# Order and costs in a planned lead-in: one transformer layer on one Trainium2 core

## The chip, the cores and the metric

The kernel runs on one core of one Trainium2 chip. The metric is the device time of one execution in microseconds; the time before is 1137.44 us, the median of 3 runs (1137.27 to 1139.29). The engines are named as the profile names them: PE (TensorE, matmuls), PEld (its weight loads), DVE (VectorE), ACT (ScalarE), POOL (GpSimd) and SP (SyncE, which issues nearly all DMAs here).

## The reference

One layer over 256 latent tokens and 256 context tokens of width 2048, in float32:

```python
sh1, sc1, g1, sh2, sc2, g2 = ada_mods(c, w_ada, b_ada)          # silu(c) @ w_ada + b_ada, in six parts
csh1, csc1, ... = ada_mods(c_ctx, w_ada, b_ada)
qa, ka, va, qb, kb, vb = mixer_qkv(x * (1 + sc1) + sh1, w_in, ...)      # one 2048 x 3072 projection, rope
qac, kac, vac, qbc, kbc, vbc = mixer_qkv(ctx * (1 + csc1) + csh1, w_in, ...)
heads = concat([window_sink_attention(qa, ka, va, kac, vac, sink),      # 8 heads, window 128, sink logit
                global_attention(qb, kb, vb, kbc, vbc)])                # 8 heads, normalised q and k
x = layer_norm(ALPHA * x + g1 * (heads @ w_out), ln1_g, ln1_b)
x = layer_norm(ALPHA * x + g2 * swiglu(x * (1 + sc2) + sh2, w_gate, w_up, w_down), ln2_g, ln2_b)
```

The feed-forward part has a hidden width of 5632. `w_ada` is 2048 x 12288, `w_in` 2048 x 3072.

## The kernel before

**Products in three parts.** Every large product is made of three matmuls on rounded float32 (`mm3`, L331 to L333): weights and activations are each split into a high part (a cast on ACT) and a low part (the rest, a subtraction on DVE), and high by high, low by high and high by low are added up in one PSUM bank. In the planned part the weights' high part is made in line L593 and the low part in L596; for the first group of activations the high part `uh` is made in L757, the whole value `uf` in L762, and the low part `ul` in L772.

**The planned part.** From the start to the beginning of the feed-forward part the program's order isn't written by hand. Each step (a DMA issue, a cast, a group of matmuls, a copy) is given to the class `Flow` with its engine, an assumed duration, the steps that it comes after, and the buffers that it takes and gives back. `Flow.search` orders the steps: it runs the list forward with ranks, gets new ranks from a backward pass, changes ranks at random (`SEED`, `MOVES`), and scores an order by `replay`, which plays it with the assumed durations and with `DRAWS` sets of durations scattered by `JITTER`. The best order is written out, one queue for each engine. On the chip each engine works through its queue in that order and waits only where data or a buffer requires it; a dependency that stands only in the plan makes no wait, only an order. The durations that matter here are `dma_ns` (L550, the rate of a load by the length of its rows), the casts (L598) and the attention's products with the values (L1097).

**The input product by groups.** The 2048 rows of `w_in` are taken in `GROUPS` of 1, 1, 2, 4 and 8 slices of 128 rows. Each group needs its columns of shift and scale first: `flow_columns` loads those columns of `w_ada` for the shift and the scale, PE multiplies them with the conditioning (L644), ACT copies the sums (L674), PE adds up the four partial rows (L679), and DVE adds the bias (L687 shift, L689 scale). `flow_part` then turns the activations round on PE (L743) and modulates them. For the first group this is done for the latent tokens (`s` = 0) and for the context (`s` = 1): `high` on ACT (L757), `whole` on DVE (L762), `rest` on DVE (L772).

`flow_blocks` loads the group's weights. A group of one slice has four pieces, of 512, 1024, 1024 and 512 columns: block 2 (keys and values of heads A, four row tiles of 128 tokens, so twelve matmuls), blocks 0 and 1, blocks 3 and 4 (queries, two row tiles each), and block 5 (keys and values of heads B). The first group's pieces go to buffers of their own (pool `b4`), all later weights to six raw buffers of 1 MB, which the columns of `w_ada` share. A raw buffer comes free when its `lo` step (L596) or its product (L644) is done, and only then can SP issue the next load for it. Around these steps PE does short products on an identity (`warm`, L381).

**After the plan** come the feed-forward loops over `w_gate` and `w_up` and over `w_down`, in an order that the tile framework keeps from the source.

Of the kernel before, what the change touches and what calls it, by code (L numbers as in the profile page):

```python
# [36 lines left out]
NB = 512  # L37
# [32 lines left out]
class Flow:  # L70
# [6 lines left out]
    OTHER = {"SP": 2000, "PE": 270, "ACT": 90, "DVE": 90, "POOL": 150}  # L77
    AGAIN = 1300
    ROUNDS = 8
    SEED, SIGMA, MOVES, DRAWS, JITTER = 312, 600.0, 800, 4, 0.03  # L80

    def __init__(self, room, begin):
        self.room, self.begin, self.steps, self.at = dict(room), begin, [], 0.0
# [173 lines left out]
def dit_layer(ctx: ExitStack, tc: tile.TileContext, x, c, cx, c_ctx, w_ada, b_ada, w_in, q_norm_g,  # L257
# [4 lines left out]
    w_ada, w_in, w_out, w_gate, w_up, w_down = (w[0] for w in (w_ada, w_in, w_out, w_gate, w_up, w_down))  # L262
# [99 lines left out]
    araw = ea.enter_context(tc.tile_pool(name="araw", bufs=ADA_BUFS))  # L362
# [146 lines left out]
    def const_tables():  # L509
        nc.gpsimd.tensor_scalar_mul(nsink, sinkb, -1.0)  # L510
        for t in range(NT):
            for g, cg, sg in ((gq, cosQ, sinQ), (gk, cosK, sinK)):
# [18 lines left out]
    F = Flow({"raw": RAW_BUFS, "araw": ADA_BUFS, "hl": HL_BUFS, "acc": 4, "wk": 4, "b4": NB4, "t2k": T2K},  # L531
             {"SP": 1800.0, "PE": 6300.0, "ACT": 5100.0, "DVE": 4200.0, "POOL": 4000.0})
# [12 lines left out]
    kv_room = [[Buf("b4") for _ in range(2)] for _ in range(2)]  # L545
# [2 lines left out]
        room.pool = "b4"  # L548

    def dma_ns(nbytes, row):  # L550
        return nbytes / (390 if row >= 2048 else 340 if row >= 1024 else 290)

    def flow_load(w, k0, nk, c0, width, where=("raw", "araw"), cut=1, small=False):
        room = Buf(*where)
# [20 lines left out]

        return room, F.add("SP", dma_ns(nk * width * P * 4, width * 4), fn, take=[room])

    def flow_weights(w, k0, nk, c0, width=NB, where=("raw", "araw"), spare=False, small=False):

        raw, ld = flow_load(w, k0, nk, c0, width, where, small=small)  # L580
        pieces = []
        for s in range(0, nk * width, SUB * NB):
            n = min(SUB * NB, nk * width - s)
            hl = Buf("b4" if spare else "hl")
            hl.rooms = [hl, Buf("b4")] if spare else [hl]

            def cast(hl=hl, s=s, n=n):
                if spare:
                    hl.hi, hl.lo = (b4([P, SUB * NB], F32R, c) for c in ("hi", "lo"))
                else:  # L590
                    hl.hi = whl.tile([P, SUB * NB], F32R, tag="hi", name="hi")
                    hl.lo = whl.tile([P, SUB * NB], F32R, tag="lo", name="lo")
                nc.scalar.copy(hl.hi[:, :n], raw.t[:, s : s + n])  # L593

            def rest(hl=hl, s=s, n=n):
                nc.vector.tensor_tensor(hl.lo[:, :n], raw.t[:, s : s + n], hl.hi[:, :n].bitcast(F32), op=ALU.subtract)  # L596

            a = F.add("ACT", 60 + 0.87 * n, cast, [ld], hl.rooms)  # L598
            b = F.add("DVE", 60 + 1.06 * n, rest, [a], give=[raw])
            pieces.append((hl, (a, b)))  # L600
        return pieces

# [26 lines left out]
    last_load, first_sum = [], []  # L629

    def flow_columns(c0, ncol, shift, scale, ats, at):

        width = ncol * P
        nk = G4 * NB // width
        ns = KD // nk
        bank, prev = Buf("wk"), None

        def fn(g, i, raw, k0, k1):
            if g == i == k0 == 0:
                bank.t = wk_bank()  # L640
            for c in range(k0, k1):
                k = g * nk + c
                j = k % 4
                nc.tensor.matmul(  # L644
                    bank.t[32 * j : 32 * j + 32, :width], lhsT=cs[:, 4 * k + 2 - 2 * i : 4 * k + 34 - 2 * i],
                    rhs=raw.t[:, c * width : (c + 1) * width],
                    start=(i == 0 and k < 4), stop=(i == 1 and k >= KD - 4),
                )

        for g in range(ns):  # L650
            F.at = ats[g]
            (r0, l0), (r1, l1) = (flow_load(w_ada, g * nk, nk, c0 + i * D, width, cut=1 if c0 else 4) for i in range(2))
            last_load[:] = [l1]
            if c0:
                def both(g=g, r0=r0, r1=r1):
                    fn(g, 0, r0, 0, nk)
                    fn(g, 1, r1, 0, nk)

                prev = F.add("PE", 1860, both, [l0, l1, prev], [bank] if g == 0 else [], [r0, r1])
            else:  # L660
                def one(i, r):
                    fn(0, i, r, 0, nk)
                    if i:
                        warm(wps.t, 2)

                prev = F.add("PE", 1080, lambda r=r0: one(0, r), [l0, prev], [bank], [r0])
                first_sum.append(prev)
                prev = F.add("PE", 1520, lambda r=r1: one(1, r), [l1, prev], [], [r1])
        F.at = at
        sb, ps = Buf("t2k"), Buf("wk")  # L670

        def copy():
            sb.t = t2k("ada")
            nc.scalar.copy(sb.t[:, :width], bank.t[:, :width])  # L674

        def sums():
            ps.t = wk_bank()
            for j in range(ncol):
                nc.tensor.matmul(ps.t[:, 4 * j : 4 * j + 4], lhsT=sb.t[:, j * P : (j + 1) * P], rhs=sel, start=True, stop=True)  # L679
            if c0 == 0:  # L680
                warm(wps.t, 4)

        def add(i):
            pv = ps.t[:, 0 : 4 * ncol].rearrange("p (j i s) -> p j i s", i=2, s=2)
            bs, bc = (bcol[:, k : k + ncol, None].to_broadcast([P, ncol, 2]) for k in (c0 // P, c0 // P + KD))
            if i == 0:
                nc.vector.tensor_tensor(shift, pv[:, :, 0, :], bs, op=ALU.add)  # L687
            else:
                nc.vector.scalar_tensor_tensor(scale, pv[:, :, 1, :], 1.0, bc, op0=ALU.add, op1=ALU.add)  # L689

        a = F.add("ACT", 60 + 0.82 * width, copy, [prev], [sb], [bank])
        b = F.add("PE", 217 * ncol - 70 if c0 else 1150, sums, [a], [ps], [sb] if c0 else [sb, wps])
        adds = [F.add("DVE", 160, lambda i=i: add(i), [(b, 0 if c0 else 1000)], give=[ps]) for i in range(2)]
        return a, adds

    u = {}
# [10 lines left out]
    def flow_part(k0, n, at, each):  # L707
# [16 lines left out]
        if k0:  # L724
            loads = [F.add("SP", max(ns, 500), load_x), F.add("SP", max(ns, 500), load_cx, take=[cx_room])]
        else:
            loads = first_sum * 2
            cx_room.pool, cx_room.t = "b4", cx0
        for s in range(2):
            F.at = at + (0.8 + 0.1 * s) * each  # L730
# [2 lines left out]
            for j0 in range(0, n, 2):  # L733
                nj = min(2, n - j0)
                ps, uf = Buf("wk"), Buf("t2k")
# [40 lines left out]
                          at=None if k0 else -1.0)  # L776
                if n == 1:
                    a = F.add("ACT", 520, high, [p] + ready, rooms)
                    b = F.add("DVE", 470, whole, [a], [uf], [ps])
                    b = F.add("DVE", 360, rest, [b], give=[uf])  # L780
                    u[k0, s][1].append((a, b))
                    continue
                for j in range(nj):
                    p = F.add("ACT", 460, lambda j=j, f=modulate: f(j), [p] + ready, [uf] if j == 0 else [], [ps])
                a = F.add("ACT", 60 + 240 * nj, cast, [p, *(c for c, _ in u[k0, s][1])], rooms if j0 == 0 else [])
                b = F.add("DVE", 60 + 330 * nj, rest, [a], give=[uf])
# [46 lines left out]
    def flow_blocks(g, bs, where=("raw", "araw")):  # L833

        k0, n = GROUPS[g]
        if n == 1:
            for i, (b0, m) in enumerate(((2, 1), (0, 2), (3, 2), (5, 1))):
                F.at = bs[0] + (bs[1] - bs[0]) * i / 4
                piece, = flow_weights(w_in, k0, 1, b0 * NB, m * NB, where if k0 else ("b4",), small=k0 == 0)
                for j in range(m):  # L840
                    flow_block(g, b0 + j, [(piece, [j * NB])])
            return
        for b in bs:
            chunks = []
            for c in range(0, n, G4):
                F.at = bs[b] + 0.01 * c
                for piece in flow_weights(w_in, k0 + c, min(n, G4), b * NB, NB, where):
                    chunks.append((piece, [0, NB]))
            flow_block(g, b, chunks)
# [142 lines left out]
    def flow_attend(gi, at, each):  # L992

        w, kb = gi // 2, gi % 2
# [3 lines left out]
        for p in range(4):  # L998
# [4 lines left out]
            pT, hx, o_ps = Buf("b4"), Buf("b4"), Buf("wk")  # L1003
# [80 lines left out]
            s = [F.add("PE", 760, lambda i=i, f=scores: f(i), qk, [banks[i]], [*qT[gi][0], *kT[w][0]]) for i in range(2)]  # L1084
            m = [F.add("DVE", 615, lambda i=i, f=largest: f(i), [s[i]]) for i in range(2)]
# [5 lines left out]
            n = [F.add("ACT", 630, lambda i=i, f=weigh: f(i), [r]) for i in range(2)]  # L1091
            g = []
            for i in range(2):
                g.append(F.add("DVE", 615, lambda i=i, f=squares: f(i), [n[i], *g], [hx] if i == 0 else [], [probs[i]]))
            a = F.add("SP", 2000, put, g, give=[hx])
            g = [(F.add("SP", 1300, get, [(a, -LANDING[0])], [pT]), -LANDING[1])]
            v = F.add("PE", 1540, values, g, [o_ps], [pT, *kv_room[w]])  # L1097
            a = F.add("ACT", 300, cast, [v, *oT[gi][1].get(0, [])[:1]], o_rooms if p == 0 else [])
            b = F.add("DVE", 350, rest, [a], give=[o_ps])
            oT[gi][1].setdefault(t, []).extend((a, b))  # L1100
# [183 lines left out]
    a = F.add("SP", 2500, const_loads, [start])  # L1284
    tables = F.add("POOL", 6000, const_tables, [a])
    for g in range(last):
        n = GROUPS[g][1]
# [83 lines left out]
    a = F.add("SP", 1000, ln_loads)  # L1371
    a = F.add("PE", 150, ln_flip, [(a, -SLACK)], [lroom])
# [433 lines left out]
```

## Time and profile before

| | |
|---|---|
| Median of 3 runs | 1137.44 us |
| The profiled execution | 1137.55 us, its span 1135.8 us |
| Instructions | 14062 |
| PE busy | 1112.2 us (98%) |
| DVE busy | 844.4 us (74%) |
| ACT busy | 551.4 us (49%) |
| Mean granted clock of PE | 0.994 |
| DMA | 321.26 MB, 283 GB/s over the span |
| Chain that ended last | PE 93%, DVE 3%, ACT 1%, DMA 1% |

The span runs from the first to the last instruction; the device time contains a little more around it. Busy times are sums over an engine's instructions without overlaps. PE's matmuls are pipelined and their ends are modelled, so that a busy PE isn't PE at its peak: whether PE runs without a break is better seen from the distance between starts. In the timeline, the last bracket of a line tells how long the engine was idle before the instruction and what ended that. "DMA share" is the mean busy share of the core's 16 DMA engines.

### The profile page before, as it was taken

How to read it: one execution, taken by the hardware profiler on the slowest of the kernel's cores; microseconds unless marked ns; L12 is line 12 of the kernel's file. 1: busy time of each engine (PE TensorE's matmuls, PEld its weight loads, DVE VectorE, ACT ScalarE, POOL GpSimd, SP SyncE). 2: the span in 40 equal slices, each digit the busy share in tenths (PEclk: the TensorE clock that was granted, in tenths of full speed). 3: DMA queues.
4: the chain of work that ended last, by engine and by line, in shares of the span. 5: the costliest groups of instructions: out<-in, count | busy, mean ns of one | idle time of the engine just before them, and what ended most of it. 6: DMA issues, size and time to landing. Idle time of an engine off the chain costs nothing.

```text
span 1135.8 us, 14062 instructions
## 1 busy us (share of the span) xinstructions
PE 1112.2 (98%) x5255; PEld 893.2 (79%) x5255; DVE 844.4 (74%) x1070; ACT 551.4 (49%) x795; POOL 41.6 (4%) x82
## 2 busy tenths in 40 slices
PE   7999999999999999999999999999999999999996
PEld 6766678778787778888888888888888888888884
DVE  4753579999999888786777566766766887686576
ACT  3341464877685356444464444444444344343442
POOL 1000050110100000010000000000000000000000
PEclk8999999999999999999999999999999999999998
DMA  9999999877999779999977677677677798887541
GB/s 292 377 379 378 377 357 361 288 249 233 336 337 377 272 261 349 317 311 328 313 213 236 224 232 241 215 256 244 226 250 254 263 376 299 315 307 261 187 148 74
DMA packets 178318, 321.26 MB, mean 283 GB/s; under 512 B 8733, under 2 KB 43197, under 8 KB 175944
## 3 DMA queue, kind: packets, MB, share of 16 engines
q1 hardware_dynamic: 177528, 320.03, 81.2%
q8 instruction: 41, 0.67, 0.2%
q10 hardware_dynamic: 720, 0.33, 0.1%
q14 instruction: 29, 0.23, 0.1%
HBM read 304.07 MB, written 16.25 MB: 282 GB/s over the span
## 4 chain that ended last, share of the span: by engine, by line
PE 93%; DVE 3%; ACT 1%; DMA 1%; issue 0%; ACTq 0%; SPq 0%; DVEq 0%
PE acc L331 28%; PE acc L333 28%; PE acc L332 28%; PE wk L644 2%; PE wk L1068 2%; PE wk L743 1%; PE wk L331 1%; DVE hx L1050 1%; PE wk L333 1%; PE wk L332 1%; DMA raw<-in_w_in_dram 1%; DMA cxt<-in_ctx_dram 0%; DVE lo L596 0%; PE wk L1401 0%; PE wk L475 0%
## 5 line engine op out<-in xcount | busy, mean ns | idle before, releaser
L322 DVE TENSOR_TENSOR lo<-raw,hi 128x1024 fp32r<-128x1024 f32 x258 | 312.8, 1221 | 167.5 <-ACT hi L321 165.0
L321 ACT CAST hi<-raw 128x1024 fp32r<-128x1024 f32 x258 | 271.7, 1055 | 335.1 <-PE acc L333 304.3
L331 PE MATMUL acc<-hi,u2h 128*128 128x512 f32 x704 | 274.6, 390 | 1.4 <-ACT u2h L1580 1.4
L333 PE MATMUL acc<-hi,u2l 128*128 128x512 f32 x704 | 274.0, 389 | 0.0
L332 PE MATMUL acc<-lo,u2h 128*128 128x512 f32 x704 | 273.9, 389 | 0.0
L331 PEld LDWEIGHTS acc<-hi,u2h 128*128 128x128 f32 x704 | 132.2, 188 | 28.8 <-ACT u2h L1580 1.6
L333 PEld LDWEIGHTS acc<-hi,u2l 128*128 128x128 f32 x704 | 132.1, 188 | 28.2 <-DVE u2l L1581 0.6
L332 PEld LDWEIGHTS acc<-lo,u2h 128*128 128x128 f32 x704 | 132.2, 188 | 27.1
L331 PE MATMUL acc<-hi,hTh 128*128 128x512 f32 x344 | 133.8, 389 | 0.4 <-ACT acc L1731 0.4
L332 PE MATMUL acc<-lo,hTh 128*128 128x512 f32 x344 | 133.9, 389 | 0.0
L333 PE MATMUL acc<-hi,hTl 128*128 128x512 f32 x344 | 133.8, 389 | 0.0
L593 ACT CAST hi<-raw 128x1024 fp32r<-128x1024 f32 (+1 forms) x86 | 87.5, 1030 | 93.0 <-DMA raw<-in_w_in_dram 42.8
L456 DVE SCALAR_TENSOR_TENSOR adav<-raw,cs,adav 128x512 f32<-128x512 f32 (+1 forms) x128 | 121.3, 947 | 11.0 <-DMA raw<-in_w_ada_dram 7.7
L596 DVE TENSOR_TENSOR lo<-raw,hi 128x1024 fp32r<-128x1024 f32 (+1 forms) x86 | 101.7, 1195 | 18.3 <-ACT hi L593 17.5
L331 PE MATMUL acc<-hi,uh 128*128 128x512 f32 x256 | 105.0, 410 | 1.0 <-ACT uh L757 1.0
L332 PE MATMUL acc<-lo,uh 128*128 128x512 f32 x256 | 101.1, 395 | 1.0 <-DVE lo L596 1.0
L333 PE MATMUL acc<-hi,ul 128*128 128x512 f32 x256 | 101.1, 395 | 0.8 <-DVE ul L772 0.8
L331 PEld LDWEIGHTS acc<-hi,hTh 128*128 128x128 f32 x344 | 64.6, 188 | 14.2 <-ACT acc L1731 0.8
L333 PEld LDWEIGHTS acc<-hi,hTl 128*128 128x128 f32 x344 | 64.6, 188 | 13.5
L332 PEld LDWEIGHTS acc<-lo,hTh 128*128 128x128 f32 x344 | 64.6, 188 | 13.5 <-DVE lo L322 0.2
L331 PEld LDWEIGHTS acc<-hi,uh 128*128 128x128 f32 x256 | 48.9, 191 | 20.4 <-issue 6.1
L333 PEld LDWEIGHTS acc<-hi,ul 128*128 128x128 f32 x256 | 48.6, 190 | 12.3 <-DVE ul L772 1.7
(224 smaller groups left out, 1147.9 us busy)
## 6 DMA issues: line engine op xcount, KB each, us to landing
raw<-in_w_ada_dram SPq DMA_DIRECT2D x70, 1024.0 KB, 6.8
raw<-in_w_gate_dram SPq DMA_DIRECT2D x44, 1024.0 KB, 5.3
raw<-in_w_up_dram SPq DMA_DIRECT2D x44, 1024.0 KB, 5.3
raw<-in_w_down_dram SPq DMA_DIRECT2D x44, 1024.0 KB, 6.5
raw<-in_w_ada_dram SPq DMA_DIRECT2D x48, 512.0 KB, 4.8
raw<-in_w_in_dram SPq DMA_DIRECT2D x18, 1024.0 KB, 6.2
raw<-in_w_out_dram SPq DMA_DIRECT2D x16, 1024.0 KB, 9.1
pd<-hx SPq DMA_DIRECT2D x64, 128.0 KB, 2.7
```

The source lines that it names most:

```text
L321: nc.scalar.copy(hi[:, :n], raw[:, s : s + n])
L322: nc.vector.tensor_tensor(lo[:, :n], raw[:, s : s + n], hi[:, :n].bitcast(F32), op=ALU.subtract)
L331: nc.tensor.matmul(ps, lhsT=xh, rhs=w[0], start=first, stop=False, skip_group_check=seeded)
L332: nc.tensor.matmul(ps, lhsT=xh, rhs=w[1], start=False, stop=False, skip_group_check=seeded)
L333: nc.tensor.matmul(ps, lhsT=xl, rhs=w[0], start=False, stop=last, skip_group_check=seeded)
L456: nc.vector.scalar_tensor_tensor(a[:, c : c + piece], raw[:, f : f + piece], cs[:, 4 * (g * (G4 * NB // w) + j) + 2, None], a[:, c : c + p ...
L593: nc.scalar.copy(hl.hi[:, :n], raw.t[:, s : s + n])
L596: nc.vector.tensor_tensor(hl.lo[:, :n], raw.t[:, s : s + n], hl.hi[:, :n].bitcast(F32), op=ALU.subtract)
L644: nc.tensor.matmul(bank.t[32 * j : 32 * j + 32, :width], lhsT=cs[:, 4 * k + 2 - 2 * i : 4 * k + 34 - 2 * i], rhs=raw.t[:, c * width : (c + ...
L743: nc.tensor.transpose(ps.t[:, (j * 2 + t) * P : (j * 2 + t + 1) * P], src, ident)
L1050: nc.vector.transpose(hx.t[:, :, i, :].rearrange("p r (k q) -> p k r q", k=4), probs[i].t.rearrange("p (k r q) -> p k r q", r=4, k=4))
L1068: nc.tensor.matmul(o_ps.t[:, : 2 * P].rearrange("p (g q) -> p g q", q=32), lhsT=v, rhs=pv[:, k], start=k == 0, stop=k == 3)
```

## The change

Four things are changed, all in what the plan is told:

- In the first group, the cast of the first weight piece comes after the copy of the conditioning sums (`first_sum[1]`), and the other three pieces' casts and low parts come after the high and the low part of the context's activations (`u[0, 1][1][0]`). The second `whole` (context) comes after the first `rest` (latents).
- `dma_ns` takes 400, 370 and 325 GB/s for rows of 2 KB and more, of 1 KB and more, and shorter ones, where it took 390, 340 and 290.
- The products with the values are taken to last 1740 ns where it was 1540.
- The search has another seed, five scattered replays for four, and a scatter of 4% for 3%.

`first_sum[:1] * 2` where it was `first_sum * 2` keeps the meaning of the line, since the list now has a second entry.

```diff
-    SEED, SIGMA, MOVES, DRAWS, JITTER = 312, 600.0, 800, 4, 0.03
+    SEED, SIGMA, MOVES, DRAWS, JITTER = 139, 600.0, 800, 5, 0.04
...
     def dma_ns(nbytes, row):
-        return nbytes / (390 if row >= 2048 else 340 if row >= 1024 else 290)
+        return nbytes / (400 if row >= 2048 else 370 if row >= 1024 else 325)
...
-    def flow_weights(w, k0, nk, c0, width=NB, where=("raw", "araw"), spare=False, small=False):
+    def flow_weights(w, k0, nk, c0, width=NB, where=("raw", "araw"), spare=False, small=False, behind=(None, None)):
...
-            a = F.add("ACT", 60 + 0.87 * n, cast, [ld], hl.rooms)
-            b = F.add("DVE", 60 + 1.06 * n, rest, [a], give=[raw])
+            a = F.add("ACT", 60 + 0.87 * n, cast, [ld, behind[0]], hl.rooms)
+            b = F.add("DVE", 60 + 1.06 * n, rest, [a, behind[1]], give=[raw])
...
         a = F.add("ACT", 60 + 0.82 * width, copy, [prev], [sb], [bank])
+        if not c0:
+            first_sum.append(a)
...
-            loads = first_sum * 2
+            loads = first_sum[:1] * 2
...
                     a = F.add("ACT", 520, high, [p] + ready, rooms)
-                    b = F.add("DVE", 470, whole, [a], [uf], [ps])
+                    b = F.add("DVE", 470, whole, [a, u[0, 0][1][0][1] if s and not k0 else None], [uf], [ps])
...
-                piece, = flow_weights(w_in, k0, 1, b0 * NB, m * NB, where if k0 else ("b4",), small=k0 == 0)
+                behind = (None, None) if k0 else (first_sum[1], None) if i == 0 else u[0, 1][1][0]
+                piece, = flow_weights(w_in, k0, 1, b0 * NB, m * NB, where if k0 else ("b4",), small=k0 == 0, behind=behind)
...
-            v = F.add("PE", 1540, values, g, [o_ps], [pT, *kv_room[w]])
+            v = F.add("PE", 1740, values, g, [o_ps], [pT, *kv_room[w]])
```

## The prediction

> **What bounds the kernel now.** I read the page first, then the busy time by stretch, the list of waits of TensorE (PE), the timeline of the first 20 us, the chain of waits, and last the DMA rate by stretch.
>
> ```profile
> span 1135.8 us, 14062 instructions
> PE 1112.2 (98%) x5255; PEld 893.2 (79%) x5255; DVE 844.4 (74%) x1070; ACT 551.4 (49%) x795; POOL 41.6 (4%) x82
> ```
>
> PE is the bound: all that the change can win is PE's idle time, 1135.8 - 1112.2 = 23.6 us, and PE time spent at a reduced clock. By stretch (columns: length, busy time of each engine with its count, granted clock, DMA share, GB/s):
>
> ```profile
> core 0: us, PE busy (x) PEld busy (x) DVE busy (x) ACT busy (x) POOL busy (x), PEclk, DMA share, GB/s
> ...
> 30.00:150.00 120.00, 120.00 (x702) 81.70 (x701) 67.45 (x98) 44.15 (x68) 0.00 (x0) 1.00 1.02 382
> 150.00:200.00 50.00, 50.00 (x228) 41.50 (x226) 46.91 (x53) 25.82 (x38) 15.11 (x16) 1.00 0.94 348
> 200.00:300.00 100.00, 96.93 (x449) 76.12 (x447) 92.60 (x181) 76.29 (x182) 14.32 (x38) 1.00 0.78 261
> ...
> 450.00:1100.00 650.00, 650.00 (x2890) 537.81 (x2889) 460.91 (x491) 297.35 (x328) 5.17 (x10) 1.00 0.78 265
> ```
>
> From 450 us on PE is never idle, and the planned part of the kernel, the only one that the change reorders, is over. From 30 to 200 us it is never idle either, so whatever PE gains before 30 us is kept to the end, provided that the loads keep up: the DMA share of 1.02 says that they have little room. In 200 to 300 us PE idles 3.07 us; its largest waits there are these (total, times, longest, us):
>
> ```profile
> PE acc L333 <- DVE oTl L1080: 1.1, 2, 0.6
> PE acc L332 <- DVE lo L596: 1.0, 1, 1.0
> ```
>
> The lead-in's waits stand in brackets in the timeline (start, duration, engine, line):
>
> ```profile
> 11.20 0.43 PE L644 MATMUL wk<-raw,cs 128*32 128x128 f32 x8 [0.32 <-DMA raw<-in_w_ada_dram]
> 11.56 0.71 PE L381 MATMUL wk<-ident 128*128 128x128 f32 x4
> 12.39 1.04 ACT L593 CAST hi<-raw 128x1024 fp32r<-128x1024 f32 x1 [2.86 <-DMA raw<-in_w_in_dram]
> 13.34 0.26 ACT L674 COPY ada<-wk 128x128 f32<-128x128 f32 x1
> 13.47 1.23 DVE L596 TENSOR_TENSOR lo<-raw,hi 128x1024 fp32r<-128x1024 f32 x1 [9.35 <-ACT hi L593]
> 13.50 0.62 ACT L593 CAST hi<-raw 128x512 fp32r<-128x512 f32 x1
> 13.66 0.39 PE L679 MATMUL wk<-sel,ada 128*128 128x4 f32 x2 [1.39 <-ACT ada L674]
> 14.49 1.05 ACT L593 CAST hi<-raw 128x1024 fp32r<-128x1024 f32 x1 [0.38 <-DMA raw<-in_w_in_dram]
> 14.61 0.15 DVE L689 SCALAR_TENSOR_TENSOR scc<-wk,bcol 128x2 f32<-128x2 f32 x1
> 14.75 2.05 DVE L596 TENSOR_TENSOR lo<-raw,hi 128x512 fp32r<-128x512 f32 x2
> 15.45 1.02 ACT L757 ACTIVATE uh<-wk,shc,scc 128x256 fp32r<-128x256 f32 x2
> 16.06 0.80 PE L331 MATMUL acc<-hi,uh 128*128 128x512 f32 x1 [1.02 <-ACT uh L757]
> 16.72 0.99 DVE L762 TENSOR_SCALAR uf<-wk,scc,shc 128x256 f32<-128x256 f32 x2
> 17.62 0.75 DVE L772 TENSOR_TENSOR ul<-uf,uh 128x256 fp32r<-128x256 f32 x2
> 18.09 0.80 PE L333 MATMUL acc<-hi,ul 128*128 128x512 f32 x1 [0.81 <-DVE ul L772]
> ```
>
> PE's sums for the conditioning end at 11.63 (11.20 + 0.43). The copy L674 that carries them on starts only at 13.34, because the cast of a 1024-wide weight piece stands ahead of it on ACT. `uh` starts at 15.45, when the next cast ends, though its scale (14.61 + 0.15) and shift stood at about 14.8. On DVE two `lo` steps of weights stand ahead of `uf`, and both `uf` ahead of the first `ul`. So PE runs without a break only from 18.09 on.
>
> **The change, part by part.** No instruction is added or removed, only the order in which the plan writes them out; the count stays at 14062.
>
> *Ordering in the lead-in.* The first piece's cast now follows the copy L674, the other three casts follow the second `uh`, their `lo` steps follow the second `ul`, and the second `uf` follows the first `ul`. Working forward from 11.63 with the durations above: the copy ends at 11.63 + 0.26 = 11.9; the sums L679 stand behind the four warming products (11.56 + 0.71 = 12.27) and end at 12.66; the two additions (0.2, from 14.61 to about 14.8 before) at 12.9; the first `uh` (1.02 / 2) at 13.4; `uf` (0.5) at 13.9; `ul` (0.4) at 14.3. That is the early end, with the first piece (512 wide) there by 12. The trace shows only that it had landed by 13.50. If it lands no sooner, its cast ends at 14.1 with `uh` behind it at 14.6, its `lo` at 14.9 (2.05 - 1.23 = 0.82), `uf` at 15.4 and `ul` at 15.8. So unbroken running starts between 14.3 and 15.8 where it was 18.09. I take 14.8, nearer the early end: the 1024-wide piece landed at 12.39 as first of its queue, and one half as wide in that place lands no later. Shift 3.3 us (2.3 to 3.8).
>
> The price is on the other three pieces. Early case: the second `uh` ends at 13.9, the next cast at 14.95, the second `ul` at 15.2, the next `lo` at 16.4. The first piece's twelve products (four row tiles by three) cover that: two before 14.3 and ten of 0.23 us (row below) end at 16.6. Cover 0.2 us; if it is gone, PE waits a few tenths once. The two pieces after that have 1.8 us and more. Behind the delayed casts only copies out of PSUM queue on ACT, and those wait for PE themselves. On SP nothing is queued behind these steps: the four pieces have buffers of their own.
>
> *The clock.* PE's clock falls in this gap. First by stretch, then in the chain of waits:
>
> ```profile
> 14.00:16.00 2.00, 1.04 (x9) 0.85 (x8) 1.86 (x5) 1.62 (x4) 0.00 (x0) 0.96 1.16 350
> 16.00:18.10 2.10, 1.23 (x3) 0.51 (x3) 2.10 (x5) 0.47 (x2) 0.00 (x0) 0.50 1.08 339
> 18.10:22.50 4.40, 4.40 (x10) 3.46 (x11) 2.94 (x5) 0.62 (x1) 0.00 (x0) 0.50 1.07 341
> ```
>
> ```profile
> 22.30 0.43 PE acc L333
> ...
> 23.00 0.23 PE acc L332
> ```
>
> From 18.89 to 22.7 nine products take 0.43 us each and afterwards 0.23. With the idle times of 1.39 and 1.02 us gone I expect the clock to stay at 1.0: 9 x 0.20 = 1.8 us more. PE could so be 3.3 + 1.8 = 5.1 us ahead at 23 us (4.1 to 5.6). The Trainium skill (TensorE: Matmul & The Clock Gate, Part 1) lets the clock fall only after a whole idle window of about 3.4 us; here no gap is longer than 1.39 us and it fell, so the trace does not agree. By that rule the 1.8 us would not be tied to the gaps and PE would be 3.3 us ahead.
>
> *What the loads allow.* PE can't keep 5.1 us if weights don't come sooner. DMA by stretch:
>
> ```profile
> 25.00:28.00 3.00, 3.00 (x53) 2.41 (x55) 2.55 (x4) 1.93 (x3) 0.00 (x0) 1.00 0.39 131
> 28.00:30.00 2.00, 2.00 (x36) 1.58 (x27) 1.23 (x1) 0.56 (x2) 0.00 (x0) 1.00 0.97 294
> 30.00:60.00 30.00, 30.00 (x195) 21.77 (x194) 22.95 (x39) 10.48 (x17) 0.00 (x0) 1.00 1.04 384
> ```
>
> The DMA engines are full apart from a hole at 25 to 30 us, where SP waited for buffers that PE and DVE had not yet let go. An earlier PE closes it: 3.0 x (1 - 131/384) + 2.0 x (1 - 294/384) = 2.0 + 0.5 = 2.45 us. To that comes the slack of the tightest weights before the next hole:
>
> ```profile
> 44.59 1.82 DVE L596 TENSOR_TENSOR lo<-raw,hi 128x1024 fp32r<-128x1024 f32 x2
> ```
>
> ```profile
> 47.21 0.49 PE L331 MATMUL acc<-hi,uh 128*128 128x512 f32 x1
> ```
>
> The last `lo` of the second group's weights ends at 46.41 and its twelve products start at 47.21: 0.8 us. So the loads allow 2.45 + 0.8 = 3.25 us, less than the 5.1 that PE could use. This is the term I take: 3.25 us.
>
> *Load rates 400/370/325 for 390/340/290, and 1740 for 1540 ns for the attention's values.* No cost in instructions. They decide what the plan takes to be in time. 384 GB/s with full queues lies between old and new for long rows. I cost this, the new seed and the wider scatter at zero, with bounds from the one stretch where order makes PE wait: half of its 3.07 us either way, 1.5 us.
>
> Sum, against the profiled execution (1137.55 us with a span of 1135.8): 1137.55 - 3.25 = 1134.3. The median of the runs is 1137.44, 0.11 lower, so the forecast for the median is **1134.2**; with the bound of 1.5 us, 1132.7 to 1135.7.
>
> **The rivals.** *The hole in the DMA stays.* The new order may again put casts behind copies that wait for PE, so that the buffers come free no sooner. Then only the 0.8 us of slack is won: 1136.6. For it: the plan is free to do so, since the new ordering concerns the first group alone. Against: the same steps that free those buffers hang on PE products that come 3 us earlier.
>
> *The attention's waits go as well.* Truer times for the values let the new plan remove the 3.07 us in 200 to 300 us: 1137.44 - 3.25 - 3.07 = 1131.1. Against it: DVE is 92.60 us busy of 100 there.
>
> *Loads later than planned: slower.* The plan now takes 1.05 MB at 400 GB/s, 2.62 us. The trace gave 382 GB/s in 30 to 150 us (2.74 us; 120 us carry 43.7 such loads, 5.4 us late) and 348 in 150 to 200 us (3.01 us; 16.6 loads, 6.5 us late): 11.9 us if no buffer absorbs any of it. Half of it would show in PE as 5.95 us: 1137.44 - 3.25 + 5.95 = 1140.1. It decides from 3.25 / 11.9 = 27% on. Against it: at a planned 390 GB/s PE lost nothing in 170 us. The Trainium skill (DMA: Bandwidth & Descriptors, Specifications) puts HBM's limit for a core at about 358 GB/s, which would speak for it; the row with 384 shows more than that limit, so the trace does not agree.
>
> **How the numbers follow.** Forecast 0.52, the hole stays 0.18, waits go as well 0.18, loads too late 0.12. A measurement of this kernel can tell about 0.2% (2.3 us) from no change, so faster means below 1135.2. The forecast's own range crosses that: I count 0.42 of its 0.52 as faster and 0.10 as the same. Faster 0.42 + 0.18 = 0.60, same 0.10 + 0.18 = 0.28, slower 0.12. The range leaves out the slower case (0.12) and the outer part of the best one (0.08): 1130.9 to 1137.6.
>
> **What would show it.** Right: the copy L674 directly behind the sums near 11.9 and ahead of every cast; first `ul` before the second `uf`; unbroken products from 14.3 to 15.8 at 0.23 us each with a clock of 1.0; no stretch near 131 GB/s at 25 to 28 us; PE's idle time before 20 us down by about 3 us. Wrong: PE waiting on `hi` or `lo` between 25 and 60 us (the loads took the gain), a clock of 0.50 after 16 us (not the gaps), or new waits on DVE in 200 to 300 us larger than 3.07 us.

## The result and the profile after

| | median, us | lowest to highest, runs |
|---|---|---|
| Before | 1137.92 | 1137.27 to 1142.47, 5 |
| After | 1133.72 | 1132.04 to 1134.73, 5 |
| Ratio | 0.9955 | 95% interval 0.9933 to 0.9976 |

By the medians the change makes the kernel 4.2 us faster (0.37%); by the ratio, which isn't that of the medians, 0.45% or 5.1 us. The forecast was 1134.2 us, 3.25 us below the 1137.44 known then. The profiled execution after took 1133.72 us. Its first page:

```profile
span 1131.9 us, 14059 instructions
PE 1112.0 (98%) x5255; PEld 891.9 (79%) x5255; DVE 843.7 (75%) x1070; ACT 551.7 (49%) x795; POOL 43.2 (4%) x82
```

The counts on all five engines are as before, so is PE's busy time, and the span is 3.9 us shorter. The three instructions fewer are semaphore instructions (1029 in the trace, where there were 1032); the prediction had the count unchanged. The lead-in in the timeline after (start, duration, engine; line numbers from L693 on are higher by 2, so that `uh` is L759, `uf` L764, `ul` L774):

```profile
10.99 0.43 PE L644 MATMUL wk<-raw,cs 128*32 128x128 f32 x8 [0.33 <-DMA raw<-in_w_ada_dram]
11.48 0.27 ACT L674 COPY ada<-wk 128x128 f32<-128x128 f32 x1 [2.02 <-PE wk L644]
11.89 0.29 PE L679 MATMUL wk<-sel,ada 128*128 128x4 f32 x2
12.31 0.62 ACT L593 CAST hi<-raw 128x512 fp32r<-128x512 f32 x1 [0.56 <-DMA raw<-in_w_in_dram]
12.84 1.01 ACT L759 ACTIVATE uh<-wk,shc,scc 128x256 fp32r<-128x256 f32 x2
13.57 0.54 DVE L764 TENSOR_SCALAR uf<-wk,scc,shc 128x256 f32<-128x256 f32 x1
14.15 0.42 DVE L774 TENSOR_TENSOR ul<-uf,uh 128x256 fp32r<-128x256 f32 x1
14.49 0.54 DVE L764 TENSOR_SCALAR uf<-wk,scc,shc 128x256 f32<-128x256 f32 x1
14.62 0.51 PE L333 MATMUL acc<-hi,ul 128*128 128x512 f32 x1 [0.41 <-DVE ul L774]
14.84 2.52 ACT L593 CAST hi<-raw 128x1024 fp32r<-128x1024 f32 x3 [0.99 <-DMA raw<-in_w_in_dram]
17.28 0.50 PE L332 MATMUL acc<-lo,uh 128*128 128x512 f32 x1
```

The copy L674 now follows PE's sums at once (11.48, it was 13.34) and the first cast stands behind it. The first `ul` runs before the second `uf`, and the 1024-wide casts come after both `uh`. PE runs without a break from 14.62 on, where it was 18.09, until a wait of 0.59 us for a load at 22.18. The stretches after (columns as in the prediction):

```profile
16.00:18.10 2.10, 2.10 (x10) 1.34 (x9) 2.10 (x3) 2.10 (x4) 0.00 (x0) 1.00 1.11 322
18.10:22.50 4.40, 3.72 (x53) 2.46 (x56) 3.85 (x7) 0.23 (x1) 0.00 (x0) 1.00 1.06 316
25.00:28.00 3.00, 3.00 (x16) 2.52 (x15) 1.65 (x3) 1.64 (x3) 0.00 (x0) 1.00 1.09 383
28.00:30.00 2.00, 2.00 (x18) 1.42 (x20) 1.14 (x4) 1.14 (x3) 0.00 (x0) 1.00 1.05 392
200.00:300.00 100.00, 99.23 (x463) 79.03 (x462) 94.59 (x184) 77.25 (x183) 14.82 (x38) 1.00 0.78 259
300.00:350.00 50.00, 48.43 (x207) 38.47 (x206) 44.93 (x62) 36.50 (x65) 0.00 (x0) 1.00 0.99 349
350.00:450.00 100.00, 97.48 (x468) 77.36 (x467) 89.42 (x127) 47.00 (x69) 4.56 (x9) 1.00 0.83 303
```

From 16.0 to 18.1 us ten products run at a clock of 1.00 where three ran at 0.50. The hole in the loads is gone: 383 and 392 GB/s where there were 131 and 294. In 200 to 300 us PE idles 0.77 us in place of 3.07, but it idles 1.57 us in 300 to 350 us, where it never did before. For the last two stretches the rows of before are:

```profile
300.00:350.00 50.00, 50.00 (x219) 40.91 (x218) 46.89 (x64) 37.66 (x67) 0.00 (x0) 1.00 0.99 348
350.00:450.00 100.00, 96.67 (x465) 77.11 (x464) 89.81 (x128) 48.03 (x70) 3.55 (x9) 1.00 0.87 312
```

So PE's idle time in 200 to 450 us falls from 3.07 + 0 + 3.33 = 6.40 to 0.77 + 1.57 + 2.52 = 4.86 us.

**PE's lead.** One measure serves all that follows. PE's products are added up from the start of a trace, each by about the time that one of its kind takes at the full clock (0.228 us for most of those with 512 columns; the short warming ones are left out). For a moment of the first profile of before, the lead is how much sooner another execution had done as much. Where the orders differ, the products at one moment are of different kinds, so values at 45 and 200 us are good to a few tenths and single values between 200 and 430 us to about 1 us; the last column has no such doubt. Each row is one execution, not a median: that of the ordering alone is the slowest of eleven, that of before with the lead-in moved the second fastest of twelve.

| Lead, us, at | 22 | 45 | 200 | 300 | 460 |
|---|---|---|---|---|---|
| after | 5.2 | 3.4 | 3.1 | 5.8 | 4.1 |
| after, taken again | 5.9 | 3.7 | 3.2 | 6.5 | 5.1 |
| before, taken again | 0.5 | 0.8 | 0.1 | -5.3 | -5.3 |
| before, lead-in moved | 5.2 | 2.7 | 2.7 | 2.3 | 2.3 |
| after, lead-in put back | -0.4 | -1.0 | -1.1 | 1.4 | 0.3 |
| ordering alone, searched anew | 4.0 | 2.3 | 2.1 | -1.5 | -9.4 |
| all but the ordering | 3.4 | 3.0 | 1.8 | 6.2 | 4.9 |
| rates and 1740 alone | 0.1 | -0.7 | -0.7 | 2.1 | 2.8 |
| seed, draws, scatter alone | 3.5 | 2.8 | 0.4 | 3.1 | 4.0 |
| all but the ordering, lead-in moved | 5.8 | 3.1 | 2.0 | 6.4 | 4.8 |

Of after's 4.1 us, 3.1 stand at 200 us, all of it won in the lead-in; about 1.0 comes later. That accounts for the shorter span. Whether the edits to the lead-in are what the time hangs on is another question, and the experiments answer it differently.

### The profile page after: what moved, and what is told of

Read it like the earlier page. It is cut to its first block, busy times and chain, and to the rows that moved or that the text cites. A ratio compares the mean times of both kernels' runs of the same rounds, so it can differ in the third digit from the quotient of the medians.

```text
span 1131.9 us, 14059 instructions
## 1 busy us (share of the span) xinstructions
PE 1112.0 (98%) x5255; PEld 891.9 (79%) x5255; DVE 843.7 (75%) x1070; ACT 551.7 (49%) x795; POOL 43.2 (4%) x82
## 4 chain that ended last, share of the span: by engine, by line
PE 79%; DMA 9%; DVE 7%; ACT 2%; issue 2%; SPq 1%; POOL 0%; ACTq 0%; DVEq 0%; POOLq 0%
PE acc L331 24%; PE acc L333 24%; PE acc L332 24%; DMA raw<-in_w_ada_dram 5%; PE wk L644 2%; DMA raw<-in_w_in_dram 1%; DVE adav L456 1%; PE wk L1071 1%; DVE g1b L456 1%; DVE lo L596 1%; DVE lo L322 1%; DMA pd<-hx 1%; DMA raw<-in_w_out_dram 1%; DMA pT<-pd 1%; PE wk L331 0%
```

## The experiments

The first theory (A) is the prediction's: the time comes from the lead-in's order, and the rest of the new plan is worth 1.5 us at most either way. Its rival (B): the new search brings a better order from 200 us on, and the lead-in adds little.

**Lead-in moved.** The plan of before stays as it was searched; only the steps of the first group change places, queue by queue, to the order that they have in after. (The function `moved` and its tables of that order are left out of the diff.)

```diff
...
-        for s, s.start, pools in self.search()[0]:
+        for s, s.start, pools in self.moved(self.search()[0]):
```

> The kernel before with its own plan; only the steps of the first group (loads, casts, low parts, activations, products, copies) are put, queue by queue, into the order that they have in the changed kernel; every other step keeps its place. Theory A (the lead-in's order makes the gain, capped by the loads): about 3.2 us faster than before (2.5 to 3.8), PE's clock stays at 1.0 after 16 us, PE 5 us ahead at 22 us and 3 us ahead from 45 us on, and the DMA hole at 25 to 28 us is gone. Theory B (the gain comes from the newly searched order of the rest): within 0.8 us of before.

Measured: 1138.70 us (1134.07 to 1143.28, 12 runs) beside 1141.04 of before (28 runs), ratio 0.998 [0.9965, 0.9995], or 2.3 us. Two stretches:

```profile
18.10:22.50 4.40, 2.37 (x10) 1.99 (x11) 2.97 (x6) 1.59 (x3) 0.00 (x0) 1.00 1.07 343
25.00:28.00 3.00, 3.00 (x39) 2.40 (x30) 1.88 (x2) 1.32 (x3) 0.00 (x0) 1.00 1.04 357
```

The clock stays at 1.00 and the hole is filled (357 GB/s). But PE is busy for only 2.37 of 4.40 us in the first row. Its wait there (total, times, longest), and then what ACT did (line numbers of this kernel are higher by 32):

```profile
PE acc L363 <- ACT kvacc L857: 2.1, 1, 2.1
```

```profile
18.97 0.62 ACT L625 CAST hi<-raw 128x512 fp32r<-128x512 f32 x1 [2.33 <-DMA raw<-in_w_in_dram]
19.50 1.07 ACT L857 COPY kvacc<-acc 128x512 f32<-128x512 f32 x2
```

A copy that frees a PSUM bank for PE stands on ACT behind the cast of a piece that hasn't landed: ACT waits 2.33 us for the load, and PE 2.1 us for the copy. So the lead of 5.2 us at 22 us falls to 2.7: a load takes it, through a queue that works in order. The lead-in by itself is so worth 2.7 us at 200 us of the trace and 2.3 us timed. The interval of the timing, 0.6 to 4.0 us, holds the 3.25 of the forecast and just reaches the 0.8 that B allowed; the trace is what speaks for A. Theory A's part of the lead-in holds, a little smaller than forecast.

**Lead-in put back.** The opposite: after's plan, with the steps of the first group in the order of before. The new dependencies, which stand in the plan only, are dropped for these steps. (The diff is against after, with the same parts left out.)

```diff
...
-        for s, s.start, pools in self.search()[0]:
+        for s, s.start, pools in self.moved(self.search()[0]):
```

> The changed kernel with its own plan; only the steps of the first group are put back, queue by queue, into the order that they had before. Theory A: about 1 us faster than before (what the rest of the new order brought from 160 us on), so 3 us slower than the changed kernel; the copy of the conditioning sums waits behind a cast again and the clock falls to 0.5 near 16 us. Theory B: 3.5 to 4.2 us faster than before, as the changed kernel.

Measured: 1137.29 us (1133.55 to 1140.34, 11 runs), ratio 0.9973 [0.9958, 0.9988]. The half clock is back where it was:

```profile
16.35:23.17 6.82, 5.93 (x13) 4.25 (x14) 5.05 (x9) 1.03 (x4) 0.00 (x0) 0.50 1.09 336
```

By the traces the lead-in is worth 3.1 + 1.1 = 4.2 us at 200 us in this plan, and 3.8 at 460. But without it the plan is timed 3.1 us faster than before (1.4 to 4.8), where A left it 1 us. So both theories have a part, and A's second half, that the rest is worth little, is in doubt.

**Ordering alone.** Before with the new dependencies only; the search runs anew with the old seed, rates and values' duration. (The diff is against after.)

```diff
-    SEED, SIGMA, MOVES, DRAWS, JITTER = 139, 600.0, 800, 5, 0.04
+    SEED, SIGMA, MOVES, DRAWS, JITTER = 312, 600.0, 800, 4, 0.03
...
+        return nbytes / (390 if row >= 2048 else 340 if row >= 1024 else 290)
...
+            v = F.add("PE", 1540, values, g, [o_ps], [pT, *kv_room[w]])
```

> The changed kernel with the seed, the draws, the scatter, the load rates and the values' duration of before: the ordering alone, with a new search. Theory A: 3.2 us faster than before, give or take 1.5 us for an order of the rest that is new again. Theory B: within 1.5 us of before.

Measured: 1143.79 us (1141.47 to 1147.09, 11 runs), ratio 1.0024 [1.0009, 1.0038]: slower by 2.7 us, where A said faster. The lead-in did its work (2.1 us ahead at 200 us) and in the profiled execution, of 1147.09 us, the rest lost 11.5 us. PE's largest waits (total, times, longest) and two stretches of this kernel:

```profile
PE acc L332 <- DVE lo L596: 3.0, 2, 2.2
PE wk L1435 <- DVE xt L1218: 2.5, 1, 2.5
```

```profile
235.97:242.79 6.82, 5.96 (x17) 4.28 (x17) 5.13 (x13) 3.45 (x16) 0.00 (x0) 0.50 0.77 244
410.05:416.87 6.82, 6.82 (x22) 5.61 (x21) 3.12 (x8) 2.82 (x8) 0.95 (x1) 0.50 0.40 146
```

PE waits for DVE, and behind such waits its clock is halved, here for 6.82 us at a time. A gain made before 30 us is not kept to the end when the order behind it is drawn anew.

**All but the ordering.** Before with the new seed, draws, scatter, rates and 1740 ns, without the new dependencies.

```diff
-    SEED, SIGMA, MOVES, DRAWS, JITTER = 312, 600.0, 800, 4, 0.03
+    SEED, SIGMA, MOVES, DRAWS, JITTER = 139, 600.0, 800, 5, 0.04
...
+        return nbytes / (400 if row >= 2048 else 370 if row >= 1024 else 325)
...
+            v = F.add("PE", 1740, values, g, [o_ps], [pT, *kv_room[w]])
```

> The kernel before with the new seed, draws, scatter, load rates and values' duration, without the ordering in the lead-in. Theory A: within 1.5 us of before, with the lead-in as before (unbroken products from about 18 us, the clock at 0.5 after 16 us). Theory B: 3 to 4.5 us faster than before.

Measured: 1133.16 us (1132.67 to 1134.31, 5 runs), ratio 0.9932 [0.9919, 0.9946], or 7.8 us, the largest gain of all. A fails here too. The timeline shows why the ordering is not needed, and the stretch from 200 us on what else was won:

```profile
12.15 0.26 ACT L674 COPY ada<-wk 128x128 f32<-128x128 f32 x1
14.44 0.50 PE L331 MATMUL acc<-hi,uh 128*128 128x512 f32 x1 [0.60 <-ACT uh L757]
16.48 0.50 PE L333 MATMUL acc<-hi,ul 128*128 128x512 f32 x1 [1.30 <-DVE ul L772]
```

```profile
200.00:300.00 100.00, 100.00 (x472) 80.63 (x471) 91.96 (x181) 78.59 (x186) 15.47 (x38) 1.00 0.78 256
```

The search put the copy early by itself (12.15 for 13.34), unbroken products start at 16.48, and PE is never idle in 200 to 300 us.

**Which edit, and what is slow in before?** Before took 1141.04 us in these comparisons, 3.6 more than its first median. So it was profiled once more, unchanged, beside its variants with one edit each. Theory E: the truer rates and the truer duration make the better order. Theory F: any edit draws another order, and before's is a poor one in its middle.

> The kernel before, unchanged, for a second profile of it. In the 28 timed runs beside the first four experiments its mean granted clock went from 0.987 to 0.995, and the slower a run the lower its clock. Theory C (stretches at half clock between 200 and 430 us cost the time): whenever the mean clock is under 0.993 the trace shows a clock of 0.5 for one or more stretches of about 3.4 us between 200 and 430 us, next to PE idle times of 0.5 us and more, and PE falls behind the first profile there by about half of their length. Theory D (loads that come later cost it): PE falls behind through waits for loads or casts before 200 us, at full clock.

Measured: 1142.85 us. It is instruction by instruction the program of the first profile (1137.55 us). The two agree within 0.1 us from 50 to 200 us; this one then falls 5.3 us behind by 260 us and stays there. The timeline shows the start of it:

```profile
180.94 1.28 DVE L456 SCALAR_TENSOR_TENSOR g1b<-raw,cs,g1b 128x1024 f32<-128x1024 f32 x1 [1.29 <-DMA raw<-in_w_ada_dram]
201.35 0.44 PE L924 MATMUL wk<-ident,kvacc 128*128 128x128 f32 x2 [0.99 <-DVE qTl L980]
238.13 0.50 PE L331 MATMUL wk<-kTh,qTh 128*128 128x512 f32 x1 [1.40 <-DVE qTl L980]
```

DVE waits 1.29 us for a load of `w_ada` that cost the first profile no wait, and the loads behind it come later as well, since their buffers come free later (SP issues the next one at 184.58 us, where it was 183.29). In 150 to 260 us DVE waits for `w_ada` four times here (first line) and once in the first profile (second line; total, times, longest):

```profile
DVE g1b L456 <- DMA raw<-in_w_ada_dram: 4.6, 4, 1.9
DVE g1b L456 <- DMA raw<-in_w_ada_dram: 1.2, 1, 1.2
```

PE then waits for DVE's `qTl` twice, 0.99 + 1.40 = 2.4 us, where it waited 0.42 us in the first profile. The second wait falls into a stretch in which DVE is busy nearly all the time and PE isn't. Two stretches of this execution, then the same two of the first profile of before:

```profile
236.40:239.80 3.40, 1.64 (x8) 0.78 (x6) 3.37 (x7) 3.25 (x14) 0.00 (x0) 1.00 0.73 237
239.80:246.60 6.80, 6.14 (x15) 4.56 (x16) 6.59 (x12) 2.43 (x12) 0.00 (x0) 0.50 0.62 196
```

```profile
236.40:239.80 3.40, 2.38 (x12) 1.63 (x10) 3.37 (x7) 3.40 (x17) 0.00 (x0) 1.00 0.60 175
239.80:246.60 6.80, 6.80 (x35) 5.54 (x34) 6.36 (x15) 5.44 (x15) 0.41 (x1) 1.00 0.74 270
```

With PE busy for 1.64 of 3.40 us the clock is halved for the next 6.8 us, and 15 products run where there were 35; with 2.38 it is not. The late loads so cost about 2.0 us of waits (2.4 - 0.4), and the other 3.3 of the 5.3 us fit the half clock, which over 6.8 us costs 3.4 at most. Theory C's halved clock is there, and what sets it off is D's late load. Among the 28 runs of before that were timed together, those with a mean clock of 0.989 or less took 1141.9 to 1143.3 us and those with 0.994 or more took 1136.5 to 1139.3. Over all 56 timed runs of before the time rises by about 0.9 us for each 0.001 that the mean clock is lower; 0.001 is 2.3 us at the half clock, so 1.1 us at most. This fits theory C for the slow runs that have no trace, but doesn't show it.

*The rates and the 1740 ns alone* (before, with those two lines of the change):

> The kernel before with the new load rates and the new duration of the values' products alone; old seed, draws and scatter, no ordering in the lead-in. Theory E (truer durations make the better plan): 4 to 8 us faster than before, as e4_plan_alone. Theory F (which of many orders the search draws decides, and any edit draws again): somewhere from 6 us faster to 4 us slower, without relation to the rates; the lead-in may be long or short.

Measured: 1134.13 us (1133.60 to 1134.84, 6 runs), ratio 0.9949 [0.9934, 0.9964], or 5.8 us beside 1140.90 of before (11 runs). The lead-in is that of before, half clock and all; the whole lead comes after 200 us.

*Seed, draws and scatter alone* (before, with that one line of the change):

> The kernel before with the new seed, draws and scatter alone; old rates, old duration of the values' products, no ordering in the lead-in. Theory E: within 2 us of before. Theory F: anywhere from 6 us faster to 4 us slower.

Measured: 1133.83 us (1132.11 to 1136.10, 6 runs), ratio 0.9945 [0.9926, 0.9964], or 6.3 us. Here the search found an early lead-in by itself (3.5 us ahead at 22 us), gave most of that back by 200 us and won 3.6 us behind. With old rates it is as good as with new ones: theory E, which had 2 us at most here, falls. F fits, at the edge of its range.

*After, unchanged, beside them:*

> The changed kernel, unchanged, timed beside the others on one chip. Theory C: 4 to 8 us faster than before, the more the lower the clock of before's runs is, with its own clock at 0.996 or more; within 1 us of e4_plan_alone's 1133.16 us, since the lead-in of that one is nearly as short. Theory A (the lead-in's order makes the gain): at least 1 us faster than e4_plan_alone.

Measured: 1132.71 us (1128.54 to 1137.34, 6 runs), ratio 0.9934 [0.9912, 0.9957], or 7.5 us. By the medians after gained 4.2 us first and 8.2 here. Of the 4.0 us between them 3.0 are before's, whose median rose (1137.92 to 1140.90), and 1.0 after's, which fell. All but the ordering had 0.9932 beside other runs of before, and theory A's 1 us over its 1133.16 did not come: the ordering adds nothing to it that these runs can tell.

**Is it that one place?** Theory C: most of before's loss is the half clock after 239.8 us, and six short products ahead of the second group's first scores would keep the clock up there.

```diff
+                if gi == 1 and t == h0 == i == 0:
+                    warm(s_ps[:, :P], 6)
```

> The kernel before with six more products on the identity (output unused), put on PE ahead of the first score product of the second query group, where the second profile of before had PE idle for 1.40 us near 237 us, at the start of its 6.83 us at half clock. Theory C (that idle time drops the clock there): the median falls by 1.5 to 2.8 us and the mean granted clock of the runs rises to about 0.994, though PE does about 1 us more work. Theory D (the half clock there has another cause, or costs nothing): 0.5 to 1.5 us slower, clocks as before.

Measured: 1139.56 us (1135.08 to 1142.86, 12 runs) beside 1140.58 of before (17 runs), ratio 0.9997 [0.9979, 1.0015]. The expected gain did not come, but this test doesn't reach theory C. In the trace the added products (the profile counts each as two) themselves wait for DVE's `qTl`, as the score product did, so that they run behind the idle time and not in it:

```profile
236.83 1.58 PE L381 MATMUL wk<-ident 128*128 128x128 f32 x12 [1.47 <-DVE qTl L980]
```

The profile, of an execution of 1138.4 us, shows the clock at 1.00 around that place, so what the slower runs of it lost their time to is not seen. The next kernel's trace shows at least that the place is not the only one.

**An extra load, before and after.** If after the change the loads set PE's pace (theory A1), then 512 KB more behind the first group's last piece must delay PE in after and hardly in before, whose loads have a hole at 25 us. In both, a part of `x` is loaded once more than needed.

```diff
                 if c0 == 5 * NB:
+                    nc.sync.dma_start(xt[:, :, 8 * P : 12 * P], x[:, 8 * P : 12 * P].rearrange("(t p) d -> p t d", p=P))
```

> The kernel before with one more load of 512 KB (columns of x that are loaded again later), issued right behind the last weight piece of the first group. At 384 GB/s it takes the DMA queues 1.37 us. Theory A1 (in the kernel before PE's order sets the lead-in and the loads have a hole at 25 to 28 us): the hole takes it up, and PE is at most 0.4 us later at 45 us than in a profile of before. Rival (loads set the pace already): 1.0 to 1.4 us later.

Measured: one execution, 1143.0 us. At 45 us PE is 0.8 us later than in the first profile of before, 1.6 later than in the second, and 0.7 later than in the kernel with the filler, whose order is before's up to there. That lies between what the two theories expect, or beyond the rival, by which profile one takes. The load went into the hole (first line, 332 GB/s for 131):

```profile
25.00:28.00 3.00, 3.00 (x70) 2.33 (x69) 2.55 (x4) 1.64 (x2) 0.00 (x0) 1.00 1.02 332
403.56:406.97 3.41, 1.47 (x9) 1.24 (x9) 2.58 (x6) 0.86 (x3) 0.00 (x0) 1.00 0.57 222
406.97:413.80 6.83, 6.83 (x21) 5.63 (x21) 3.91 (x10) 3.00 (x6) 0.95 (x1) 0.50 0.50 154
```

The other two lines show a second place of before's order where PE is busy for less than half of 3.41 us (1.47) and the clock is halved for the next 6.83. It waits there 1.94 us for DVE (`xt`). The same wait, in the trace of before with the lead-in moved, leaves the clock at 1.00:

```profile
398.50:401.91 3.41, 1.47 (x10) 1.32 (x10) 2.46 (x5) 0.98 (x3) 0.00 (x0) 1.00 0.53 205
401.91:408.70 6.79, 6.78 (x34) 5.44 (x33) 5.42 (x12) 5.16 (x10) 0.96 (x1) 1.00 0.48 155
```

So such a place costs time in some executions and not in others. From 30 to 460 us the traces with before's order show no half clock in the executions of 1137.55 and 1138.4 us (the second with the filler), 6.8 us in that of 1142.85, and 3.4 + 6.8 in this one of 1143.0. Those of after, taken twice, and of the four other plans that were timed 5.8 us faster or more show none.

> The changed kernel with the same load of 512 KB in the same place. Theory A1 (with the new order the loads set PE's pace from 22 us to 50 us): PE is 1.0 to 1.4 us later at 45 us than in the profile of the changed kernel, by a longer wait for the second group's columns of w_ada near 22 us. Rival (PE's own order still sets it): at most 0.4 us later.

Measured: one execution, 1136.27 us. PE is 3.1 us later at 30 us than in after's profile and 2.9 at 45 and at 200: more than twice the 1.0 to 1.4 of A1. Two stretches:

```profile
18.10:25.00 6.90, 4.38 (x73) 2.96 (x72) 3.60 (x7) 0.00 (x0) 0.00 (x0) 1.00 1.10 342
25.00:28.60 3.60, 3.60 (x10) 2.81 (x9) 1.29 (x2) 1.39 (x4) 0.00 (x0) 0.53 1.09 384
```

The load delays the second group's `w_ada`, PE idles 2.52 us in 18.1 to 25.0 (0.68 without the extra load), and then the clock is halved for 3.4 us as well, which about doubles the price. So after the change the loads do set the pace here: the direction is A1's, the size is not. For before the answer stays open.

**Both together.** All but the ordering, with the lead-in's steps moved as in the first experiment: the version that the findings point to.

> e4_plan_alone with the steps of the first group put, queue by queue, into the order that they have in the changed kernel. Its unbroken products should start near 14.6 us instead of 16.5. Theory A1: PE is about 3 us ahead of the first profile of before at 200 us, where e4_plan_alone was 1.8 us ahead, and the time is 1 us below e4_plan_alone's, 0.8% to 1.0% below before in the same call. Rival (the lead is given back by 200 us): within 0.5 us of e4_plan_alone's lead.

Measured: 1133.42 us (1130.59 to 1136.17, 6 runs), ratio 0.9942 [0.9919, 0.9964]; no better than all but the ordering (0.9932) or after (0.9934). The rival holds: 2.0 us ahead at 200 us, beside 1.8 without the move. The lead is 5.8 us at 22 us for 3.4 without the move, but 3.1 for 3.0 at 45 us. Two stretches show where most of it goes:

```profile
28.00:30.00 2.00, 1.34 (x18) 0.42 (x16) 1.63 (x4) 0.96 (x3) 0.00 (x0) 1.00 1.04 391
30.00:45.00 15.00, 14.37 (x101) 10.23 (x102) 11.58 (x20) 6.04 (x9) 0.00 (x0) 1.00 1.07 398
```

The largest wait of PE there:

```profile
PE wk L676 <- DMA raw<-in_w_ada_dram: 0.9, 1, 0.9
```

PE idles 0.66 + 0.63 = 1.29 us in 28 to 45 us, most of it for a load, with the loads at 391 and 398 GB/s; without the move it doesn't idle there. Of the 2.4 us that the move gives at 22 us next to nothing is left at 45; the other 1.1 us don't show as a wait.

## Why the prediction was right, and where it was not

**Start of the unbroken products.** Taken 14.8, measured 14.62. The bet that the first piece lands by about 12 held: its cast starts at 12.31, on the landing. The product that needs the second piece's low part starts at 17.28 without a wait, so the cover of 0.2 us was enough. What was said to be harmless behind the delayed casts, "only copies out of PSUM", was so in after; with the lead-in moved by hand just such a copy cost 2.1 us.

**The clock.** It stayed at 1.00, and PE was 5.2 us ahead at 22 us where 5.1 was said. In the lead-in moved and in after the half clock went with the gaps, and with the gaps put back it came back. All six profiles with the old order in the lead-in have 6.8 us of it there, none of the eight others has any between 8 and 25 us. So the 1.8 us are tied to the gaps, though not by the length of a gap alone: with the lead-in moved PE waits 2.06 us near 19 us, longer than any gap in before's lead-in, at a clock of 1.00.

**The loads.** The hole closed (383 GB/s where 131 was), and the lead shrank from 5.2 to 3.1 us at 200 us; 3.25 was worked out. In after's trace one wait for a load is seen behind 18 us:

```profile
PE wk L644 <- DMA raw<-in_w_ada_dram: 0.6, 1, 0.6
```

That is 0.6 of the 2.1 us given back; a wait of 0.3 us is for a copy on DVE (`qacc`), and for the rest the trace shows no wait. That loads set the pace is better shown by the kernel with an extra load, and by the two kernels with the steps moved by hand, where PE's largest losses behind 18 us (2.1 and 0.9 us) end with a landing, the first by way of ACT. So the size of the term was right, and its reason is shown in part.

**The step that was mis-sized** is "I cost this, the new seed and the wider scatter at zero", with its bounds of 1.5 us. In after it happened to be worth 1.0 us by the trace; after's plan without the lead-in's order was timed 3.1 us faster than before. By itself the term measured 5.8 us (rates and 1740 ns), 6.3 us (seed, draws, scatter) and 7.8 us (all of them) faster, and in the search with the new dependencies and the old seed it went the other way: 2.7 us slower, with 2.1 us ahead at 200 us ending as 9.4 us behind in the slowest run. The bound had been taken from the waits of one profiled execution, 3.07 us. It missed that a new search draws another order of everything from 30 to 450 us, and that a wait there can be followed by 6.8 us at half the clock, which more than doubled its price in the second profile of before.

**A sentence that fell** with it: that "whatever PE gains before 30 us is kept to the end". It holds only for an order that is kept, as when the steps were moved by hand (2.7 us at 200 us, 2.3 at 460), and not for one that is searched anew.

**The rivals.** The hole did not stay. The attention's waits went in part (3.07 to 0.77 us), and 1.57 us of new ones came in the next 50 us. Loads later than planned did not show: from 18 to 200 us PE waits for one load, 0.6 us, and its waits in 300 to 450 us, the largest 1.4 us, are for ACT and DVE.

**What the forecast could not see** is that the 1137.44 us it started from was low for before: its later medians were 1140.6 to 1141.0. The second profile shows one cause, loads that come late with no slack behind them and a halved clock. So the same change measured 4.2 and 8.2 us by the medians. The forecast was worked out from an execution of before whose planned part has no halved clock behind the lead-in. That the time after came within 0.5 us of it is in part luck, since the term put at zero could have gone either way by several us. The 3.25 us were right for the lead-in; the ordering is however not what the faster kernel needs, since the new plan alone does as well.

**Open.** Why the orders with new rates or with the new seed are both better from 200 us on isn't settled: beside after's own, four searches with some edit were tried, three came out 5.8 to 7.8 us faster and one 2.7 slower, which fits chance draws around a poor order but doesn't prove it. By the traces the three are 2.8 to 4.9 us ahead of an execution of before without a halved clock behind 30 us; that they have none either, where before's order has it in some executions, may be the rest. Nor is it shown what most of before's slower runs lose their time to: two traces show the halved clock, the other runs have only their lower mean clock, and the filler did not fill the idle time that it was meant for.

## What to carry to other kernels

In a queue that works in order, look for a long step that stands ahead of a short one on the critical path. Moving it is worth what the next limit allows, here the loads, and that limit has to be priced too. Where an edit makes a planner search anew, the search is an edit of its own that can outweigh the intended one: test the intended part with the rest of the order held fixed, and the search with the intended part left out. Choose between plans by several executions, since in a part without slack loads that come a little late, and the halved clock behind them, cost 5.3 us here between two executions of one program.

## What the runs showed of the hardware

In every trace the changes of the granted clock lie whole multiples of 3.41 us apart (in the ordering alone at 235.97, 242.79, 307.64, 311.06, 410.05 and 416.87 us), and the halved stretches inside the program lasted 3.41 or 6.83 us. It was halved after such steps of 3.41 us in which PE was busy 1.47 and 1.64 us, and was kept after one with 2.38 us; in the one with 1.64 the longest wait was 1.40 us. Busy time doesn't decide alone: with the same wait of 1.94 us and the same 1.47 us of work the clock was halved in the kernel with an extra load and kept in the one with the lead-in moved, and it was halved after 1.99 us of work at 11.11 to 14.52 us in the second profile of before. The Trainium skill (TensorE: Matmul & The Clock Gate, Part 1) has the clock fall after an idle window of about 3.4 us; the traces agree with 3.4 us, but not with PE having to be idle for the whole of it.

The same program, instruction by instruction, took 1137.55 and 1142.85 us; the difference began with one load for which DVE waited 1.29 us, and grew by later waits for loads and by 6.8 us at the half clock. With queues full, DMA moved 391 to 398 GB/s over 17 us (all but the ordering, lead-in moved).
